# Value products of two attention units in one block, a fourth buffer for turned probabilities, and small tables in another pool

## The chip, the core and the metric

The kernel runs on one NeuronCore of a Trainium2 chip, in one launch. The time is the device time of one execution in microseconds (us); a kernel is run several times and the median counts. The profile is that of one execution, taken by the hardware profiler; its span goes from the first to the last instruction. The engines have their own instruction streams: TensorE (PE in the profile, with its weight loads listed as PEld), VectorE (DVE), ScalarE (ACT), GpSimd (POOL) and SyncE (SP), whose queue issues nearly all DMAs here.

## What is computed

One layer of a diffusion backbone over 1024 latent tokens (a grid of 16 rows of 64 columns) and 256 context tokens, width 1024, all in float32. The normalised and modulated tokens go through one input projection; its output feeds two groups of heads. The first is neighbourhood attention: 8 heads of 64, each query sees a window of 8 rows by 16 columns around it and all context keys in one softmax. The second is a gated delta scan: 4 heads of 128, in two directions, in chunks. Both are gated, put side by side, and sent through the output projection.

```python
def row_block(r):                       # one grid row of queries
    k_win = k_rows[:, :, col_idx]
    v_win = v_rows[:, :, col_idx]
    s_loc = jnp.einsum('bchd,bicjhd->bhcij', q_r, k_win) + bias
    s_ctx = jnp.einsum('bchd,bnhd->bhcn', q_r, k_ctx)
    p = softmax(concatenate([s_loc, s_ctx]))
    return (jnp.einsum('bhcij,bicjhd->bchd', p_loc, v_win)
            + jnp.einsum('bhcn,bnhd->bchd', p_ctx, v_ctx))
...
y = concatenate([o_na * silu(na_z), o_g * silu(g_z)]) @ w_out
x = x + gate * rmsnorm(y, g_post)
```

## The kernel before

The kernel goes through five stages. The first (`phase0`, L194) loads the small tables and the first weights, makes the modulation vectors and the first projections. The second (`phase2`) and third (`phase_a2`) run the other projections, the short convolutions and the preparation of the delta scan. The fourth, `phase_b` (L1492), runs the attention and the scan together. The last, `phase4`, is the output projection; it takes in the tail of the scan.

**Attention.** A unit is 128 queries (8 rows by 16 columns) of two heads; there are 32 units (`units`, L621: 4 pairs of heads, 2 halves of the grid, 4 column groups). The loop of `na_attn` (L665) takes one head of one unit per step, so 64 steps and three more. In step i it does, in this order:
- `na_scores`: the products of queries and keys into the one PSUM tile `sc` (L751 for context, L754 for the window), the masking and row maximum on VectorE (L758), the exponential on ScalarE (L759);
- from step 3 on, in every odd step, `values` (L625), which calls `na_values` for one unit: products of the turned probabilities of both heads with the values, into `po`. One head writes partitions 0 to 63, the other 64 to 127, by half-width tiles of the array (`tile_position=(0, hb)`): 4 products for the context (L784) and 6 for the window (L789). After every fourth unit the sum is multiplied into the gate (L632) and the reciprocal of the softmax sums is spread out (L634 to L639);
- a part of the scan;
- `na_turn` for the step before: five transposes on TensorE into `tc` (L768) and `tr` (L772), copied by ScalarE to `tcx` (L770) and `tl` (L775), of which there are three buffers each;
- after every fourth unit `end`, which turns the reciprocals and multiplies again (L645, L647);
- another part of the scan.

**The scan.** `delta_step` (L1222) has three parts for each step of both directions: L1242 (product with the state) with y on VectorE (L1244); L1260 (product with y) with vn on ScalarE (L1263, L1265); L1271 (update of the state) and, for the outputs, L1249 and L1282. Each needs the result of the one before. The loop in `phase_b` (L1503 to L1506) places just under two such parts in each step of the attention.

**What sets the order.** The matmuls of the attention and scan are chained to each other in program order by `pe` (L594), so their order on TensorE is that of the code. The other engines' order comes from a planner, which simulates the program. Buffers are given out per pool and tag: a tile waits until the readers of the tile that had its place are done.

**Pools.** `cp` (left) and `np` (right) live through the whole kernel; `hp` (left) holds the normalised tokens and is given back after the third stage; `nw` (left) holds the attention's small tiles and opens after that. The constant table `c128` has the identity, two triangles for running sums (`tri_u`, `tri_l`, used in `gate_prep`, L990) and a selector (`sel`).

Of the kernel before, what the change touches and what calls it, by code (L numbers as in the profile page):

```python
# [11 lines left out]
F32 = mybir.dt.float32  # L12
# [8 lines left out]
P = 128  # L21
# [18 lines left out]
def host_consts():  # L40
    ident = np.eye(P, dtype=np.float32)
    i = np.arange(P)
    tri_u = (i[:, None] <= i[None, :]).astype(np.float32)
    tri_l = (i[:, None] >= i[None, :]).astype(np.float32)
    masks = []
    a = np.arange(P) // 16
    c = np.arange(P) % 16
    for rt in range(2):
        r = 8 * rt + a
        rs = np.clip(r - 4, 0, 8)  # L50
        krow = 4 * rt + np.arange(12)
        rok = (krow[None] >= rs[:, None]) & (krow[None] < rs[:, None] + 8)
        for ct in (0, 1, 3):
            q = 16 * ct + c
            cs = np.clip(q - 8, 0, 48)
            kcol = KCOL0[ct] + np.arange(NCOLS[ct])
            cok = (kcol[None] >= cs[:, None]) & (kcol[None] < cs[:, None] + 16)
            ok = rok[:, :, None] & cok[:, None, :]
            m = np.where(ok, np.float32(0), np.float32(NEG))
            masks.append(m.reshape(P, 3, 4, -1).transpose(0, 1, 3, 2).reshape(P, -1))  # L60
    t = np.arange(S)
    row = (t // 64).astype(np.float32)
    col = (t % 64).astype(np.float32)
    inv = np.float32(10000.0) ** (-np.arange(0, 64, 2, dtype=np.float32) / np.float32(64))
    inv = inv.astype(np.float32)
    ar = (row[:, None] * inv[None]).astype(np.float32)
    ac = (col[:, None] * inv[None]).astype(np.float32)
    cr, sr, cc, sc = (f(z.astype(np.float64)).astype(np.float32)
                      for z, f in ((ar, np.cos), (ar, np.sin), (ac, np.cos), (ac, np.sin)))
    tok = lambda z: z.reshape(8, P, -1).transpose(1, 0, 2).reshape(P, -1)  # L70
    rope = np.concatenate([tok(np.concatenate([cr, cc], 1)), tok(np.concatenate([-sr, sr, -sc, sc], 1))], 1)
    sel = (i[:, None] % 32 == np.arange(2)[None, :]).astype(np.float32)
    c128 = np.concatenate([ident, tri_u, tri_l, sel], axis=1)
    return {
        "c128": np.ascontiguousarray(c128),
        "masks": np.concatenate(masks, axis=1).astype(ml_dtypes.bfloat16),
        "rope": np.ascontiguousarray(rope),
    }
# [63 lines left out]
class K:  # L142
# [31 lines left out]
    def setup(self, ctx):  # L174
        tc, nc, I = self.tc, self.nc, self.I
        self.cp = ctx.enter_context(tc.tile_pool(name="cp", bufs=1, side="left"))
        self.dp = ctx.enter_context(tc.tile_pool(name="dp", bufs=1, space=DRAM))
        cp = self.cp
        c128 = cp.tile([P, 3 * P + 2], F32, name="c128")
        nc.sync.dma_start(c128, I["c128"])  # L180
        self.ident = c128[:, 0:P]
        self.tri_u = c128[:, P:2 * P]
        self.tri_l = c128[:, 2 * P:3 * P]
        self.sel = c128[:, 3 * P:3 * P + 2]
        self.cols = cp.tile([P, 117], F32, name="cols")
        self.gg_dram = self.dp.tile([1, D], F32, name="gg_dram")
        self.nwh = cp.tile([P, 1], F32, name="nwh")
        self.ones = cp.tile([P, 1], F32, name="ones")
        nc.gpsimd.memset(self.ones, 1.0)
        self.mhalf = cp.tile([P, 1], F32, name="mhalf")  # L190
        nc.gpsimd.memset(self.mhalf, -0.5)


    def phase0(self):  # L194
        tc, nc, I = self.tc, self.nc, self.I
        cp = self.cp
# [3 lines left out]
        self.chl = self.hp.tile([P, KC, CT], F32R, name="chl")  # L200
        np_, vp, ps = self.np, self.vp, self.ps
        self.v_dram = self.dp.tile([4, 64, 4, 512], F32, name="v_dram")
        self.gates = np_.tile([P, 10, 16], F32, name="gates")
        self.vcx = np_.tile([P, 2, 512], F32, name="vcx")
        with tc.tile_pool(name="p0", bufs=1, side="right", reuse_waits="tile") as p0:
            vt = p0.tile([P, P], F32, name="vt")
# [4 lines left out]
            nc.vector.tensor_copy(cols, pv[:, :117])  # L211
            nc.vector.tensor_scalar(self.nwh, cols[:, 116:117], 0.5, None, ALU.mult)
            th = p0.tile([P, 16], F32, name="th")
            sc = self.sc = self.np.tile([P, 8, 32], F32, name="sc")
            nc.gpsimd.memset(sc, 0.0)
            nc.scalar.activation(th, cols[:, 0:16], AF.Tanh, scale=0.5)
            nc.vector.tensor_scalar(th, th, 0.5, 0.5, ALU.mult, ALU.add)
# [139 lines left out]
            gates = [self.gate_proj(vp, ps, 0, 1536, gate_w(1536))]  # L357
# [39 lines left out]
        f = self.I["rpbp"]  # L397
# [88 lines left out]
    def values(self, pool, w, n, tiles):  # L486

        for t in tiles:
            sel = self.nat_tok(t - 2) if t >= 2 else self.ctx_tok(t)
            pv = self.ps.tile([P, 512], F32, name=f"pv{t}_{n}", tag="pj", bufs=3)  # L490
            self.mm_tok(pv[:, :264], w, 0, 264, sel)
            self.values_out(t, n, pv)
# [106 lines left out]
    def na_attn(self, na, ps):  # L599


        nc = self.nc
# [62 lines left out]
        for i in range(2 * len(units) + 3):  # L665
            if i < 2 * len(units):
                j, hh = divmod(i, 2)
                p, rt, ct = units[j]
                if (ct, hh) == (0, 0):
                    sums[p, rt] = self.nw.tile([P, 4, 2], F32, name=f"sums{p}_{rt}", tag="sums", bufs=2)  # L670
                scores[i] = self.na_scores(ps, p, rt, ct, hh, pairs[p], sums[p, rt])
                if p < 3 and (rt, ct, hh) == (0, 2, 0):
                    self.gate = self.scan_loads
                    pairs[p + 1] = load(p + 1)
                    self.gate = None
            if i >= 3 and i % 2:
                values((i - 3) // 2)
            yield
            if 1 <= i <= 2 * len(units):
                turned[divmod(i - 1, 2)] = self.na_turn(ps, *scores.pop(i - 1))  # L680
            if i >= 4 and i % 8 == 2:
                end((i - 4) // 2)
            self.split_piece(1, 2)
            yield
# [78 lines left out]
    def na_turn(self, ps, nm, m, pt):  # L763
        nc = self.nc
        pc = ps.tile([P, 256], F32, name=f"tc{nm}", tag="tc", bufs=1)
        pl = ps.tile([P, 384], F32, name=f"tr{nm}", tag="tr", bufs=1)
        for cc in range(2):
            self.pe(nc.tensor.transpose(pc[:, cc * P:(cc + 1) * P], pt[:, 384 + cc * P:384 + (cc + 1) * P], self.ident))  # L768
        tcx = self.nw.tile([P, 2, P], F32, name=f"tcx{nm}", tag="tcx", bufs=3)
        nc.scalar.copy(tcx.rearrange("p c q -> p (c q)"), pc)  # L770
        for rc in range(3):
            self.pe(nc.tensor.transpose(pl[:m, rc * P:(rc + 1) * P], pt[:, 384 + (rc - 3) * m:384 + (rc - 2) * m],  # L772
                                        self.ident))
        tl = self.nw.tile([P, 384], F32, name=f"tl{nm}", tag="tl", bufs=3)
        nc.scalar.copy(tl[:m, :], pl[:m, :])  # L775
        return tl, tcx

# [779 lines left out]
```

## Time and profile before

| what | us |
|---|---|
| runs: lowest, median, highest | 875.4, 877.32, 1006.16 |
| span of the profiled execution | 869.9 |
| TensorE busy in the span | 824.9 |
| VectorE, ScalarE, GpSimd busy | 502.7, 417.3, 357.3 |

For the profiled execution only its span is listed; the time of a run is measured around it, and the lowest of the runs is 5.5 us above the span. A matmul's busy time overlaps the next one's, so TensorE's busy share says little of how densely it issues; the start times of its instructions do. A row of the timeline merges neighbouring instructions of one line: start, duration of the whole, engine, line, operation, output and inputs, count, and in brackets the idle time of that engine before it and what ended it.

### The profile page before, as it was taken

Reading aid. Unit: us, or ns where it says so; the run is one execution under the profiler, and the core shown is the slowest. Engines: PE = TensorE matmul, PEld = TensorE weight load, DVE = VectorE, ACT = ScalarE, POOL = GpSimd, SP = SyncE. Lnnn points to the kernel's source line nnn. Section 1 sums busy time; section 2 is a strip of 40 time slices with the busy share of each in tenths; the row PEclk is TensorE's granted clock in tenths of the full one; section 3 lists DMA queues with packets and bytes.
Section 4 is the critical chain, followed back from the end, with each engine's and each line's share of the span. In section 5 each row is a group of like instructions: output and inputs, shape, how many; then the busy total and the mean of one; then the engine's idle time right before and its main releaser. Section 6 shows DMA issues by size and latency. Waiting matters only on the chain.

```text
span 869.9 us, 16461 instructions
## 1 busy us (share of the span) xinstructions
PE 824.9 (95%) x6082; PEld 696.4 (80%) x6082; DVE 502.7 (58%) x1051; ACT 417.3 (48%) x1087; POOL 357.3 (41%) x430
## 2 busy tenths in 40 slices
PE   6999999999999989989898999899999999999996
PEld 3678887888788867769786788788898988878885
DVE  3444455536743699859935964456666655653342
ACT  5244334753664643355314334366666667734210
POOL 2224141453462553328262100655757559624110
PEclk9999999999999999989998999699999999999999
DMA  8778352255444825562597569995967925134251
GB/s 340 265 259 295 97 170 88 73 170 168 142 157 154 221 85 170 176 171 81 176 283 226 160 187 290 419 258 149 313 179 262 259 78 191 49 110 133 87 184 69
DMA packets 86054, 159.65 MB, mean 184 GB/s; under 512 B 18373, under 2 KB 45334, under 8 KB 83798
## 3 DMA queue, kind: packets, MB, share of 16 engines
q1 hardware_dynamic: 78486, 144.94, 53.0%
q10 hardware_dynamic: 7488, 13.67, 5.1%
q8 instruction: 48, 0.79, 0.4%
q14 instruction: 32, 0.26, 0.1%
HBM read 109.51 MB, written 52.42 MB: 186 GB/s over the span
## 4 chain that ended last, share of the span: by engine, by line
PE 59%; DVE 16%; DMA 15%; issue 4%; ACT 2%; POOL 2%; SPq 1%; DVEq 0%; POOLq 0%; ACTq 0%
PE py L1369 3%; PE py L1370 3%; PE py L1371 3%; DVE tb L1078 3%; DVE vb L1081 3%; PE pa L1260 2%; PE pz L463 2%; PE pz L468 2%; PE pz L467 2%; PE po L789 2%; DMA wada<-in_w_ada 2%; PE pa L1271 2%; PE po L784 2%; DMA pm_dram<-pm 2%; PE tr L772 2%
## 5 line engine op out<-in xcount | busy, mean ns | idle before, releaser
L759 ACT ACTIVATE pt<-pt,nm 128x544 f32<-128x544 f32 (+1 forms) x64 | 50.5, 790 | 37.5 <-DVE nm L758 37.0
L758 DVE CUSTOM_DVE_ANT_0 pt<-sc,gm 128x544 f32<-128x544 f32 (+1 forms) x64 | 49.4, 771 | 32.2 <-PE sc L754 25.8
L742 POOL TENSOR_TENSOR gm<-gt,mk 128x288 f32<-128x288 f32 (+1 forms) x48 | 46.5, 971 | 29.1 <-DVE nm L758 28.8
L1232 POOL TENSOR_SCALAR kd<-kt,kd 128x128 f32<-128x128 f32 x72 | 42.7, 605 | 20.5 <-PE pa L1271 19.9
L1020 ACT ACTIVATE em<-em,gc 128x128 f32<-128x128 f32 x80 | 25.5, 391 | 34.9 <-DMA em<-gc_dram 29.7
L467 PE MATMUL pz<-hl,wh_gz 128*128 128x512 f32 x96 | 38.6, 402 | 0.0
L463 PE MATMUL pz<-hh,wh_gz 128*128 128x512 f32 x96 | 38.3, 399 | 0.0
L468 PE MATMUL pz<-hh,wl_gz 128*128 128x512 f32 x96 | 38.2, 398 | 0.0
L476 PE MATMUL pv<-wh_nv,hh 128*128 128x264 f32 x128 | 35.5, 296 | 2.0 <-ACT hh L265 1.7
L477 PE MATMUL pv<-wh_nv,hl 128*128 128x264 f32 x128 | 36.8, 292 | 0.0
L1431 DVE TENSOR_TENSOR finv<-py,ggb 128x512 f32<-128x512 f32 x16 | 10.9, 689 | 43.2 <-ACT finv L1430 43.1
L478 PE MATMUL pv<-wl_nv,hh 128*128 128x264 f32 x128 | 35.6, 287 | 0.0
L1274 DVE SCALAR_TENSOR_TENSOR s<-s,egl,pa 128x128 f32<-128x128 f32 x64 | 19.6, 344 | 27.2 <-PE pa L1271 27.2
L1039 POOL TENSOR_SCALAR_AFFINE_SELECT qe<-qe 128x256 f32<-128x256 f32 x32 | 25.5, 800 | 24.1 <-DVE qe L1038 24.1
L887 DVE SCALAR_TENSOR_TENSOR acc_v<-xp_v,cols,acc_v 128x1282 f32<-128x1282 f32 x16 | 29.1, 1817 | 10.9 <-ACT acc_v L885 10.6
L1078 DVE TENSOR_TENSOR tb<-ab,vb 120x31 f32<-120x31 f32 (+15 forms) x62 | 30.2, 487 | 8.7 <-DMA ab<-ab_dram 7.1
L1137 POOL COPY tm<-ld 32x320 f32<-32x320 f32 x16 | 7.4, 464 | 65.0 <-DMA tm_dram<-tm 27.1
L1430 ACT ACTIVATE finv<-py 128x512 f32<-128x512 f32 x16 | 9.5, 597 | 48.6 <-PE py L1371 30.5
L1238 POOL TENSOR_SCALAR vb<-v,beta 128x128 f32<-128x128 f32 x40 | 24.2, 604 | 20.4 <-DVE y L1244 17.2
L772 PE MATMUL tr<-c,pt 128*96 128x128 f32 (+1 forms) x192 | 31.8, 275 | 0.0
L1035 DVE SCALAR_TENSOR_TENSOR pm<-pk,beta,em 128x128 f32<-128x128 f32 x80 | 23.5, 342 | 14.0 <-PE pk L1028 10.9
L770 ACT COPY tcx<-tc 128x256 f32<-128x256 f32 x64 | 23.4, 366 | 16.2 <-PE tc L768 15.8
(432 smaller groups left out, 2852.7 us busy)
## 6 DMA issues: line engine op xcount, KB each, us to landing
wada<-in_w_ada SPq DMA_DIRECT2D x16, 512.0 KB
em<-gc_dram SPq DMA_DIRECT2D x20, 256.0 KB
pm_dram<-pm SPq DMA_DIRECT2D x20, 256.0 KB
tm_dram<-tm SPq DMA_DIRECT2D x8, 640.0 KB
kk<-qk_dram SPq DMA_DIRECT2D x16, 320.0 KB
tm<-tm_dram SPq DMA_DIRECT2D x4, 1280.0 KB
kq_dram<-kq SPq DMA_DIRECT2D x4, 1152.0 KB
kq<-kq_dram SPq DMA_DIRECT2D x4, 1152.0 KB
```

What stands on the lines that cost most here:

```text
L463: r = nc.tensor.matmul(ps, wh, xh, start=(k == 0), stop=False)
L467: nc.tensor.matmul(ps, wh, xl, start=False, stop=False)
L468: nc.tensor.matmul(ps, wl, xh, start=False, stop=(k == KC - 1))
L476: nc.tensor.matmul(ps, xh, wh, start=(k == 0), stop=False)
L477: nc.tensor.matmul(ps, xl, wh, start=False, stop=False)
L478: nc.tensor.matmul(ps, xh, wl, start=False, stop=(k == KC - 1))
L742: r = nc.gpsimd.tensor_tensor(self.gm[hh][:, 384 - n:384].rearrange("p (n c r) -> p n c r", c=nco, r=4), gv, self.mk[:, mo:mo + n].rearran ...
L758: nc.vector.tensor_tensor_reduce(pt[:, 384 - n:], sc[:, 512 - n:768], gm[:, 384 - n:], -1.0, 3.0e38, ALU.add, ALU.min, nm)
L759: self.last_exp = nc.scalar.activation(pt[:, 384 - n:], pt[:, 384 - n:], AF.Exp, bias=nm, scale=-1.0, accum_out=sums[:, ct, hh:hh + 1]).in ...
L772: self.pe(nc.tensor.transpose(pl[:m, rc * P:(rc + 1) * P], pt[:, 384 + (rc - 3) * m:384 + (rc - 2) * m], self.ident))
L1078: nc.vector.tensor_tensor(t3, bc(ab[:, 0:m, m:m + 1], [r, m, n]), bc(vb[:, m:m + 1, m:], [r, m, n]), ALU.mult)
L1232: r = nc.gpsimd.tensor_scalar(kd[d], kt_[:, t, :], self.kd[:, h, d, t:t + 1], None, ALU.mult)
```

## The change

- `na_attn`: `values` is no longer called for one unit in every odd step from 3 on, but for two units, one behind the other, in every fourth step: steps 5, 9, 13 up to 65.
- `na_turn`: four buffers instead of three for `tcx` and `tl` (2.5 KB more per partition).
- The constant table is laid out as identity, selector, triangles. The first two are loaded into `cp`, the triangles by a DMA of their own into `hp`. `gates` and the silu vector `sc` move from `np` to `hp`. (`cp` gives up 1 KB per partition, `np` 1.6 KB, `hp` takes 2.6 KB.)

```diff
-    c128 = np.concatenate([ident, tri_u, tri_l, sel], axis=1)
+    c128 = np.concatenate([ident, sel, tri_u, tri_l], axis=1)
...
-        c128 = cp.tile([P, 3 * P + 2], F32, name="c128")
-        nc.sync.dma_start(c128, I["c128"])
+        c128 = cp.tile([P, P + 2], F32, name="c128")
+        nc.sync.dma_start(c128, I["c128"][:, :P + 2])
         self.ident = c128[:, 0:P]
-        self.tri_u = c128[:, P:2 * P]
-        self.tri_l = c128[:, 2 * P:3 * P]
-        self.sel = c128[:, 3 * P:3 * P + 2]
+        self.sel = c128[:, P:P + 2]
...
-        self.gates = np_.tile([P, 10, 16], F32, name="gates")
+        self.gates = self.hp.tile([P, 10, 16], F32, name="gates")
+        tri = self.hp.tile([P, 2 * P], F32, name="tri")
+        nc.sync.dma_start(tri, I["c128"][:, P + 2:])
+        self.tri_u, self.tri_l = tri[:, :P], tri[:, P:]
...
-            sc = self.sc = self.np.tile([P, 8, 32], F32, name="sc")
+            sc = self.sc = self.hp.tile([P, 8, 32], F32, name="sc")
...
-            if i >= 3 and i % 2:
+            if i >= 5 and i % 4 == 1:
+                values((i - 5) // 2)
                 values((i - 3) // 2)
...
-        tcx = self.nw.tile([P, 2, P], F32, name=f"tcx{nm}", tag="tcx", bufs=3)
+        tcx = self.nw.tile([P, 2, P], F32, name=f"tcx{nm}", tag="tcx", bufs=4)
...
-        tl = self.nw.tile([P, 384], F32, name=f"tl{nm}", tag="tl", bufs=3)
+        tl = self.nw.tile([P, 384], F32, name=f"tl{nm}", tag="tl", bufs=4)
```

## The prediction

> **What bounds the kernel now.** I read the page first, for the share of each engine, then the windows of the attention stage, then its timeline, and last the waits of TensorE's weight loads in it.
>
> ```profile
> span 869.9 us, 16461 instructions
> PE 824.9 (95%) x6082; PEld 696.4 (80%) x6082; DVE 502.7 (58%) x1051; ACT 417.3 (48%) x1087; POOL 357.3 (41%) x430
> ...
> core 0: us, PE busy (x) PEld busy (x) DVE busy (x) ACT busy (x) POOL busy (x), PEclk, DMA share, GB/s
> 552.00:781.00 229.00, 220.38 (x2022) 199.37 (x2021) 136.11 (x414) 144.61 (x443) 140.82 (x191) 0.99 0.66 200
> ```
>
> The value products run only between 552 and 781 us of the span. There TensorE is busy for 220.38 of 229.00 us at a granted clock of 0.99, VectorE for 136.11, ScalarE for 144.61, GpSimd for 140.82. So the stage is TensorE's instruction stream, and what shortens it is time in which that stream issues nothing. The other three are busy for about 60%; they cannot bound the stage by throughput, but a late answer of theirs can stop the stream. The order of the attention's and scan's matmuls is written by hand, so the change of the loop moves them exactly as written.
>
> The stream around one block of value products (unit 24/25, the first row is a scores product of the step before, which has no such block):
>
> ```profile
> 631.05 0.30 PE L754 MATMUL sc<-kk,ql 128*128 128x288 f32 x1
> 631.18 0.66 PE L1260 MATMUL pa<-y,tm 128*128 128x128 f32 x4
> ...
> 633.93 0.30 PE L754 MATMUL sc<-kk,ql 128*128 128x288 f32 x1
> 634.16 0.42 PEld L784 LDWEIGHTS po<-tcx,vcx 128*64 128x64 f32 x8 [0.17 <-ACT o L1286]
> 634.16 0.66 PE L784 MATMUL po<-tcx,vcx 128*64 128x128 f32 x8
> 634.65 0.83 PE L789 MATMUL po<-tl,vv 96*64 96x128 f32 x12
> 635.40 0.52 PEld L1242 LDWEIGHTS pa<-s,kq 128*128 128x128 f32 x4 [0.17 <-DVE o L1290]
> 635.40 0.71 PE L1242 MATMUL pa<-s,kq 128*128 128x128 f32 x4
> ```
>
> Read the start times: from the last scores product to the next matmul it is 0.13 us without a block (631.05 to 631.18), 0.23 us into a block of half-width tiles (633.93 to 634.16). The weight loads stand still for 0.17 us at the way in, and again 0.17 us at the way out (the brackets), each time beside a releaser that has nothing to do with the operands. I take the two gaps, 0.34 us, as the price of entering and leaving the 128x64 tiles once. The block itself lasts from 634.16 to 635.40, 1.24 us.
>
> **The change, part by part.** 1. *Half the blocks.* Today there are 32 blocks of 20 value instructions (4 products of context, 6 of the window, two instructions each), one in every second step. Afterwards there are 16 blocks of 40. No matmul is added or dropped; 16 entries and exits go: 16 x 0.34 = 5.4 us off the stream. Bounds: 0 if the gap is something else (a rival below), 5.4 by these rows.
>
> 2. *The operands of a block.* Waits of the weight loads in the stage (who waited for what: us in total, times, longest us), with the group of L784 above them:
>
> ```profile
> L784 PEld LDWEIGHTS po<-tcx,vcx 128*64 128x64 f32 x256 | 13.4, 136 | 8.5 <-ACT tcx L770 2.1 <-ACT vn L1265 1.6 <-issue 1.5
> ...
> PEld pa L1260 <- DVE y L1244: 5.6, 11, 0.7
> PEld po L784 <- ACT tcx L770: 2.1, 4, 0.7
> PEld sc L751 <- DVE nm L758: 1.9, 3, 1.3
> ...
> PEld po L784 <- ACT tl L775: 1.0, 4, 0.3
> PEld po L784 <- ACT pt L759: 1.0, 2, 0.7
> PEld pa L1271 <- ACT vn L1263: 1.0, 2, 0.6
> ```
>
> A block's last operand is the turned probability of the step just before, copied out of PSUM by ScalarE. The three ScalarE rows that carry it (the two copies, and the exponential that stands ahead of them) make 2.1 + 1.0 + 1.0 = 4.1 us in 10 entries; less 0.17 us each for the entry itself, 2.4 us are real waits. In a double block the first unit's operands are two steps old and its 1.24 us cover the second unit's. So this wait goes: 2.4 us off. Bounds: 0, and 8.5 - 32 x 0.17 = 3.1 us, all idle time before L784 that is not entry.
>
> 3. *The bare steps.* What takes the place of the removed blocks is the cost. A step without a block gives VectorE and ScalarE less time. Two steps side by side, first a bare one, then one with a block:
>
> ```profile
> 651.63 0.29 PE L754 MATMUL sc<-kk,ql 128*128 128x288 f32 x1
> 651.64 0.54 PEld L1242 LDWEIGHTS pa<-s,kq 128*128 128x128 f32 x4
> ...
> 652.32 0.71 DVE L758 CUSTOM_DVE_ANT_0 pt<-sc,gm 128x544 f32<-128x544 f32 x1
> 652.96 0.34 DVE L1244 SCALAR_TENSOR_TENSOR y<-pa,nsc,v 128x128 f32<-128x128 f32 x1
> 653.22 0.34 DVE L1244 SCALAR_TENSOR_TENSOR y<-pa,nsc,vb 128x128 f32<-128x128 f32 x1
> 653.36 0.56 PEld L1260 LDWEIGHTS pa<-y,tm 128*128 128x128 f32 x4 [0.68 <-DVE y L1244]
> ...
> 634.38 0.72 DVE L758 CUSTOM_DVE_ANT_0 pt<-sc,gm 128x544 f32<-128x544 f32 x1
> 636.13 0.34 DVE L1244 SCALAR_TENSOR_TENSOR y<-pa,nsc,v 128x128 f32<-128x128 f32 x1
> 636.52 0.56 PEld L1260 LDWEIGHTS pa<-y,tm 128*128 128x128 f32 x4
> ```
>
> In the bare step the scan's first product (L1242) follows the scores at once. VectorE first masks the scores (L758, 0.71 us), and only then makes the scan's y (L1244); the scan's next product (L1260) waits for it, 0.68 us. In the step with a block (634.38 on) the masking ran under the values, y was made as soon as its product was there, and L1260 shows no wait. Today 33 of the 64 steps of scores have no block. Afterwards blocks stand only in every fourth step, so 16 steps (3, 7, ... 63) become bare. The scan has three parts per step of its own and nearly two are placed in each loop step, so L1242 comes first in about one bare step in three: 16 / 3 = 5.3 more. At the mean of the row, 5.6 / 11 = 0.51 us, that is 2.7 us. The two other answers that a bare step can wait for, the masking before the next scores (1.9 us in 3, of which one of 1.3 lies alone; I take 1.9 - 1.3 = 0.6) and the scan's vn on ScalarE (1.0 us), make 1.6 us over these 33 steps, so 0.8 us over 16 more. Together 3.5 us on. Bounds: 0, where VectorE and ScalarE find the time in the longer pause of the double block, and 16 x 0.68 = 10.9 us, where every new bare step waits as the one shown.
>
> 4. *Four buffers.* Two units wait for their products at once, so four turned tiles live. The copy into a buffer comes behind transposes that stand after the block on the same in-order stream; the block has read the buffer by then. No new wait: 0. A fifth live tile never arises.
>
> 5. *PSUM and the end.* The products of a row of four units still accumulate in one tile and are read at the same step; what follows them (the next unit's first block) comes two steps later than today, which only loosens it. At the end the block of unit 30 moves from step 63 to step 65, behind the last turn:
>
> ```profile
> 763.68 0.66 PE L784 MATMUL po<-tcx,vcx 128*64 128x128 f32 x8
> ...
> 773.63 0.66 PE L784 MATMUL po<-tcx,vcx 128*64 128x128 f32 x8
> ...
> 775.80 0.88 PE L789 MATMUL po<-tl,vv 96*64 96x128 f32 x12
> ...
> 777.85 1.77 DVE L1316 TENSOR_TENSOR o<-o,rq_y_o 128x512 f32<-128x512 f32 x1
> 779.54 0.68 DVE L632 TENSOR_TENSOR zs<-po,zs 128x512 f32<-128x512 f32 x1
> 780.37 0.63 PE L645 MATMUL prt<-c,rb 128*128 128x128 f32 x4 [1.66 <-DVE zs L632]
> ```
>
> The last block ends at 775.80 + 0.88 = 776.68, but VectorE reads it only at 779.54, behind L1316. Another 1.24 us before it is covered by that 2.86 us, and the stream is shorter by as much ahead of it. 0, with bounds 0 and +1.24.
>
> 6. *Small tables.* The table with the identity is loaded in two DMAs, and the second (128 KB of triangles) is one more issue on SyncE's queue, ahead of the vectors and of every load of the first phase:
>
> ```profile
> 0.79 0.39 SPq L180 DMA_DIRECT2D c<-in_c  x1
> 1.23 0.43 SPq L207 DMA_DIRECT2D vt<-in_vecs  x1
> ...
> 3.51 0.43 PE L209 MATMUL pv<-c,vt 117*128 117x117 f32 x1 [3.51 <-DMA vt<-in_vecs]
> 11.44 2.24 PE L294 MATMUL par<-wada,sc 128*32 128x512 f32 x8 [0.21 <-DMA wada<-in_w_ada]
> ```
>
> One issue takes 0.43 us, and everything behind it on that queue starts so much later: the vectors that L209 waits for, and the w_ada loads that the first products wait for at 11.44. The bytes are the same. I take +0.4 us; bounds 0 and +0.4. GpSimd's and ScalarE's queues are not passed. A page of the Trainium skill speaks for more: DMA: Bandwidth & Descriptors, in its part on the life of a DMA, gives every transfer a fixed cost of about 2.0 us beside its bytes at 436 GB/s. By it, if the new load stood whole on the chain, my estimate for it would be 2.3 us and the sum 1.9 us worse. The trace agrees with the size and not with the place: the vectors are there 3.51 - 1.23 = 2.28 us after their issue, but the table issued 0.44 us earlier was there by the same moment, so transfers run side by side and only the issue adds. Moving the gates and the silu vector to another pool changes no instruction.
>
> **The sum:** -5.4 - 2.4 + 3.5 + 0 + 0 + 0.4 = -3.9 us against the profiled span of 869.9, so 866.0. No time of the profiled execution is listed beside its span; the median of the runs, 877.32, lies 7.4 us above it, the lowest, 875.4, 5.5 us. I hang the difference on the median: 873.4, about 0.4% faster. What a measurement of this kernel can tell from no change is about 2%, 17.5 us.
>
> **The rivals.** *Bare steps cost nothing.* The double block leaves VectorE and ScalarE a pause of 2.5 us in every fourth step in which they catch up; for it speaks their 60% of busy time, against it the 0.68 us above, which is order on VectorE and not load. -5.4 - 2.4 + 0.4 = -7.4: 869.9.
>
> *Bare steps cost more* (the other side). Three bare steps now follow each other, and VectorE's masking stands before y in each of them: at the 0.68 us of the bare step shown, in all 16, it is +10.9 - 7.8 + 0.4 = +3.5: 880.8, slower than before. It decides from 7.4 / 16 = 0.46 us per new bare step. Against it: L1242 stands first in only a third of them. To pass 2% it would take (17.5 + 7.4) / 16 = 1.56 us per step, more than any wait of the stage's rows above.
>
> *The change does not do what it says.* If the 0.17 us gaps belong to the operands or to this particular PSUM tile, a block of 40 keeps a gap in its middle, nothing of the 5.4 us is saved: -2.4 + 3.5 + 0.4 = +1.5: 878.8. Against it the way out, where the gap stands before L1242, whose operands are a state and a key that no value product touches. A page of the Trainium skill, TensorEngine Tiling (Array Packing), under its key properties, says that a change of the tiling mode, not of the tile, drains TensorE; by that rule this rival falls and the 5.4 us stand. The two gaps of 0.17 us agree with it as far as a trace without a double block can.
>
> **How the numbers follow.** My forecast has a chance of 0.55, bare steps at nothing 0.15, bare steps dearer 0.2, gaps that stay 0.1. The predicted time is the first's, 873.4. The range goes from 868.0 (the second, with 3.1 instead of 2.4 us of operand waits, 869.2, and 1.2 us for the runs' own spread) to 882.0 (the third, 880.8, and the 1.24 us of the end). By these cases faster by over 2% would need more than all idle time priced above: 0.03. Slower by over 2% is the far end of the third: 0.04. Within 2%: 0.93.
>
> **What would show it.** In the changed profile: half as many idle gaps of 0.17 us before L784, and 40 value instructions without a gap in their middle (step 1); no row of L784 waiting for tcx or tl (step 2); L1260 waiting for y in about 16 places instead of 11 and some 2.7 us more (step 3); TensorE's idle time at the end as it is (step 5); the vectors' issue 0.4 us later (step 6). The prediction is wrong if the stage from the first scores to the last turned row does not get shorter by 3 to 6 us, or if time moves outside that stage, which only a new order of the other engines by the planner could do.

## The result and the profile after

| kernel | median us (runs) | ratio to the kernel before, 95% interval |
|---|---|---|
| before, measured beside it | 872.54 (7) | |
| changed | 879.12 (7) | 1.0077 [1.0054, 1.0100] |

The change makes the kernel about 0.8% slower, 6.6 us. That is under the 2% that the prediction set as the bound of a visible difference, but the interval leaves no doubt of the sign. The prediction said 0.4% faster.

The page and the windows of the changed kernel, for the stage from the first scores to the last turned row:

```profile
span 877.4 us, 16456 instructions
PE 829.0 (94%) x6082; PEld 704.2 (80%) x6082; DVE 504.6 (58%) x1051; ACT 417.6 (48%) x1087; POOL 359.5 (41%) x430
...
552.00:789.00 237.00, 223.12 (x2030) 203.68 (x2029) 137.64 (x416) 144.75 (x443) 141.91 (x191) 0.97 0.64 195
```

Each engine runs as many instructions as before, but the stage is 8 us longer (237 against 229 us), TensorE stands still for 13.9 us in it instead of 8.6, and its granted clock is 0.97 instead of 0.99. By three marks, the first scores product, the first product of the last step of scores and the end: 552.4, 763.0 and 869.9 before; 553.1, 771.7 and 877.4 after. So +0.7 us ahead of the stage, +8.0 in it, -1.2 behind it.

What the change was meant to do, it did. One double block in the timeline (start, duration, engine, line; from here on the rows of a timeline or of a list of waits are picked out, in their order):

```profile
640.31 0.29 PE L756 MATMUL sc<-kk,ql 128*128 128x288 f32 x1
640.54 0.66 PE L786 MATMUL po<-tcx,vcx 128*64 128x128 f32 x8
641.02 0.83 PE L791 MATMUL po<-tl,vv 128*64 128x128 f32 x12
641.68 0.61 PE L786 MATMUL po<-tcx,vcx 128*64 128x128 f32 x8
642.12 0.83 PE L791 MATMUL po<-tl,vv 96*64 96x128 f32 x12
642.87 0.71 PE L1244 MATMUL pa<-s,kq 128*128 128x128 f32 x4
```

The 40 instructions have no idle time in their middle: the second unit's L786 starts 0.66 us behind the first's L791, like any two lines of one block. From 640.54 to 642.87 it is 2.33 us, where two blocks of before took 2 x 1.24 us, each with a way in of its own ahead of it.

The waits of the weight loads in the stage show what it cost instead (waited for: us in total, times, longest):

```profile
PEld pa L1262 <- DVE y L1246: 11.0, 20, 1.0
PEld po L786 <- issue: 3.9, 17, 0.4
PEld pos L1251 <- DVE o L1292: 3.6, 4, 1.4
PEld sc L753 <- DVE nm L760: 2.2, 4, 1.3
PEld ot L1321 <- POOL o L1313: 2.1, 1, 2.1
```

No row of L786 waits for tcx or tl any more, and it has 17 short idle times. But the wait for y has doubled (5.6 us in 11 before), and two waits are new: for the scan's output o on VectorE, and for the product on GpSimd that ends a scan.

The steps of the loop can be compared one by one: from the first scores product of a step to that of the next, less 1.09 us for each unit of value products and 0.345 us for each block in it. Both come from the steps: a double block makes a step 1.09 us longer than a single one (the median of 15 steps), and in steps 7 and 15, where nothing waits, a single block makes it 1.44 us longer than none, so a block costs some 0.35 us beside its products.

| steps | changed less before, us |
|---|---|
| the newly bare ones up to the last but one (3, 7, ... 59, 15 steps) together | +5.6 |
| old bare ones: 8, 20, 24 | +1.3, +2.5, +1.9 |
| old bare ones: 16, 32, 48 | +0.3, +0.5, +0.7 |
| 21 (with a double block, at half clock) | +1.0 |
| all 63 | +13 |

Against these 13 us stand the 5 us of saved blocks. More than half of the loss (7.5 us) is in steps that had no block before either, and those the prediction had not priced at all. Two entries of the sum can't simply be put down to the double blocks: step 55 (+1.8) and step 2 (+0.6). Against the same trace of before, step 55 is 1.3 to 1.6 us longer in runs 1, 9, 11, 14 and 15 below, and step 2 is 0.8 to 1.0 us longer in runs 11, 13 and 14, all with single blocks: in these two steps that trace was a short one. Step 24, in the timeline of the changed kernel:

```profile
634.89 1.13 POOL L744 TENSOR_TENSOR gm<-gt,mk 128x384 f32<-128x384 f32 x1
634.98 0.19 ACT L761 ACTIVATION_READ_ACCUMULATOR pt<-pt,nm 128x1 f32 x1
635.20 0.86 DVE L635 TENSOR_SCALAR rs<-sums 128x8 f32<-128x8 f32 x1 [0.45 <-ACT pt L761]
635.50 0.30 PE L756 MATMUL sc<-kk,ql 128*128 128x288 f32 x1
635.97 0.34 DVE L1246 SCALAR_TENSOR_TENSOR y<-pa,nsc,v 128x128 f32<-128x128 f32 x1
636.37 0.62 PEld L1262 LDWEIGHTS pa<-y,tm 128*128 128x128 f32 x4 [0.81 <-DVE y L1246]
636.76 0.71 DVE L760 CUSTOM_DVE_ANT_0 pt<-sc,gm 128x544 f32<-128x544 f32 x1
637.61 0.29 DVE L1292 TENSOR_TENSOR o<-pos,o 128x128 f32<-128x128 f32 x1
637.96 0.52 PEld L1251 LDWEIGHTS pos<-s,kq 128*128 128x128 f32 x4 [0.97 <-DVE o L1292]
```

The doubling of the softmax sums, rs (eight numbers per partition), stands ahead of y. It waits for the exponential's sums (0.45 us) and then takes 0.86 us. It ends at 636.06, 0.04 us behind the end of GpSimd's gm (634.89 + 1.13 = 636.02). TensorE waits for y, and 1.6 us later again for o. In the trace of before the same instruction stands one step earlier, between the scan's two state updates, and meets only the end of gm:

```profile
628.48 1.14 POOL L742 TENSOR_TENSOR gm<-gt,mk 128x384 f32<-128x384 f32 x1 [1.43 <-DVE nm L758]
629.48 0.17 DVE L634 TENSOR_SCALAR rs<-sums 128x8 f32<-128x8 f32 x1
629.56 0.33 DVE L1274 SCALAR_TENSOR_TENSOR s<-s,egl,pa 128x128 f32<-128x128 f32 x1
```

Nobody wrote that move: with the value block gone from step 23, the planner found another order for VectorE. In step 20 it did the same on GpSimd. First the changed kernel, with the granted clock (the last but two of the windows' numbers) behind it, then before:

```profile
618.24 1.18 POOL L1234 TENSOR_SCALAR kd<-kt,kd 128x128 f32<-128x128 f32 x2
619.39 1.90 POOL L1313 TENSOR_TENSOR o<-o,rq_y_o 128x1024 f32<-128x1024 f32 x1
621.34 0.66 PE L1321 MATMUL ot<-c,o 128*128 128x128 f32 x4 [1.95 <-POOL o L1313]
...
622.00:624.00 2.00, 2.00 (x11) 1.56 (x11) 0.75 (x1) 0.85 (x2) 0.72 (x2) 0.50 1.00 231
```

```profile
615.85 1.90 POOL L1311 TENSOR_TENSOR o<-o,rq_y_o 128x1024 f32<-128x1024 f32 x1
617.72 1.18 POOL L1232 TENSOR_SCALAR kd<-kt,kd 128x128 f32<-128x128 f32 x2
617.93 0.60 PE L1319 MATMUL ot<-c,o 128*128 128x128 f32 x4
```

The two kd stand ahead of the product o now; TensorE waits 1.95 us for it, and is then granted half its clock.

### The profile page after: what moved, and what is told of

The parts are those of the page before. It is cut to its first block, busy times and chain, and to the rows that moved or that the text cites. A ratio compares the mean times of both kernels' runs of the same rounds, so it can differ in the third digit from the quotient of the medians.

```text
span 877.4 us, 16456 instructions
## 1 busy us (share of the span) xinstructions
PE 829.0 (94%) x6082; PEld 704.2 (80%) x6082; DVE 504.6 (58%) x1051; ACT 417.6 (48%) x1087; POOL 359.5 (41%) x430
## 4 chain that ended last, share of the span: by engine, by line
PE 67%; DVE 16%; DMA 10%; issue 3%; POOL 2%; ACT 2%; SPq 1%; DVEq 0%; POOLq 0%; ACTq 0%
PE py L1371 3%; PE py L1372 3%; PE py L1373 3%; DVE tb L1080 3%; PE pz L464 3%; PE pz L468 3%; PE pz L469 3%; PE pa L1262 2%; DVE vb L1083 2%; PE po L791 2%; DMA pm_dram<-pm 2%; PE po L786 2%; PE tr L774 2%; PE sc L756 2%; PE pos L1251 2%
## 5 line engine op out<-in xcount | busy, mean ns | idle before, releaser
L889 DVE SCALAR_TENSOR_TENSOR acc_v<-xp_v,cols,acc_v 128x1282 f32<-128x1282 f32 x16 | 29.0, 1814 | 10.9 <-ACT acc_v L887 10.6
L1433 DVE TENSOR_TENSOR finv<-py,ggb 128x512 f32<-128x512 f32 x16 | 10.9, 689 | 41.5 <-ACT finv L1432 41.5
```

## The experiments

Three theories stood at the start. **A**: the loss is the new order on VectorE and GpSimd. **B**: three bare steps in a row starve the scan's own chain, whatever the order. **C**: the moved tables and the buffers cost. Later expectations name their own. "Before" is measured beside each set of runs and lies at 872.3 to 873.1 us.

**1. The tables and buffers alone.** The changed kernel with the loop of before:

```diff
-            if i >= 5 and i % 4 == 1:
-                values((i - 5) // 2)
+            if i >= 3 and i % 2:
                 values((i - 3) // 2)
```

> The small tables in the other pool and the four buffers, with the loop of before (one unit's value products in every odd step). Theory A (the loss comes from where VectorE's and GpSimd's small operations stand once the blocks are doubled): the attention stage as before, the first phase up to 0.7 us later, time within 1 us of the kernel before. Theory C (tables or buffers cost by themselves, through the first phase or through waits for memory): 3 us or more slower than before, and the doubled blocks are innocent.

Measured: 876.45 us, 1.0048 [1.0029, 1.0066], 4 us: C's number. The stage lasts 211.5 us (before 210.6), so nearly all of it lies outside. This was a surprise, and runs 7, 11, 14 and 15 follow it up. In the profiled execution the first scores come 2.3 us later than before, and the part behind the last scores is 1.4 us longer, with half the clock from 785.3 to 788.7 us. The traces of runs 9 and 15 have that second stretch too, and their times are those of before, so it is no answer.

**2. The order on GpSimd.** The changed kernel with the two kd of step 2 of the next scan held behind the product o:

```diff
+                if h and i == 2:
+                    self.order(r, self.o_done)      # r: the kd, o_done: the product L1313
```

> The changed kernel, with one order added on GpSimd: at the end of a head the product of the outputs with their norm (1.9 us) stands ahead of the two kd products of the next head's third step, as it did before the change. Theory A: the 2.1 us wait of the transposes (ot) in step 20 goes, and with it the 3.4 us at half clock that follow it: 2 to 3.5 us faster than the changed kernel, about 876 us. Theory B (three bare steps in a row starve TensorE, whatever the order): no more than 1 us faster.

Measured: 879.22 us, 1.0085 [1.0052, 1.0117]. The stage fell from 218.6 to 215.9 us; step 20 loses 0.8 instead of 2.5 us, and step 21 ran at full clock. So the order costs what A said, inside the stage. But the total kept nothing of it, as B said. In that profile the first scores came 5.3 us later than in the changed kernel's, which hides it there; why the median of four runs shows no gain stays open.

**3. Both orders.** As 2, and rs held behind the product of the value sums, which puts it behind y and o:

```diff
+            gated = nc.vector.tensor_tensor(row(p, rt), po[p, rt]..., row(p, rt), ALU.mult)
-            nc.vector.tensor_scalar(rs, sums[p, rt]..., 2.0, None, ALU.mult)
+            self.order(nc.vector.tensor_scalar(rs, sums[p, rt]..., 2.0, None, ALU.mult), gated.ins.name)
```

> As the one with the order on GpSimd, and on VectorE the doubling of the softmax sums (rs) stands behind the product that reads the value sums, so in the step with a double block and no longer in the bare step ahead of it. Theory A: the waits of steps 8, 16, 24, 32, 48 and 55 go as well, 5 to 6 us more: about 870 us, 2 to 3 us faster than before the change. Theory B: within 1.5 us of the changed kernel, 878 us.

Measured: 879.13 us, 1.0081 [1.0054, 1.0108], stage 215.2. Steps 8, 24 and 48 lose 0.8, 0.9 and 0.3 instead of 1.3, 1.9 and 0.7, but the sum hardly moved. A's 870 was missed: these two orders are not the whole loss.

**4. The kernel before, with the order of after for rs.** rs and its reciprocal moved into the bare step, behind the last state update and ahead of y:

```diff
+            if i >= 8 and i % 8 == 0:
...
+                r = nc.vector.tensor_scalar(rs, sums[p, rt]..., 2.0, None, ALU.mult)
+                self.order(r, self.last_s)
```

> The kernel before, its blocks in every odd step, with the doubling and reciprocal of the softmax sums put into the bare step after the fourth unit's last scores (steps 8, 16, ...), ahead of that step's y on VectorE. Theory A: the place alone costs: 3 to 6 us slower than before, with L1260 waiting for y or the output products for o in those steps. Theory B: the place costs nothing without three bare steps in a row: within 1 us of before.

Measured: 872.5 us, 1.0006 [0.9980, 1.0032]; no step differs by over 0.25 us. The place of rs alone costs nothing: there it met GpSimd's kd rather than gm in five of eight places, and took 0.16 to 0.27 us in seven. That points to the meeting with gm as what costs; runs 5 and 6 test it.

**5. An addition for the doubling.** In the changed kernel rs became the sum of the sums with themselves:

```diff
-            nc.vector.tensor_scalar(rs, sums[p, rt]..., 2.0, None, ALU.mult)
+            nc.vector.tensor_tensor(rs, t, t, ALU.add)       # t: the sums
```

> The changed kernel with the doubling of the softmax sums (rs, 128x8) written as the sum added to itself, a two-operand addition, instead of a multiplication by a constant; no engine's order changes. Theory A (the constant multiplication is held up by a running GpSimd table addition, since it ended 0.03 us behind the end of gm in steps 8, 24, 48 and 55, and an addition is not): the eight take 0.16 to 0.2 us each, 1.4 in all in place of 3.6, the products y behind them come 0.4 to 0.7 earlier in four steps, and the time falls by 1.5 to 3 us, to 876 to 877.5. Rival B (they wait for the exponential's sums, or any VectorE instruction is held up so): the eight still take 0.2 to 0.9 us and the time stays at 879.

Measured: 879.2 us, 1.0071 [1.0047, 1.0095]. The addition is held up just the same (instruction, count, ns min/median/max, first and last start), so the first form of the explanation fell:

```profile
L636 DVE TENSOR_TENSOR rs<-sums x8: 164/391/853, 579.0 to 776.6; 128x8 f32<-128x8 f32 x8
```

That it is gm and not the exponential shows in the trace of run 1, step 55, where the sums had been there for 0.16 us when rs started:

```profile
738.50 0.18 ACT L760 ACTIVATION_READ_ACCUMULATOR pt<-pt,nm 128x1 f32 x1
738.53 1.13 POOL L743 TENSOR_TENSOR gm<-gt,mk 128x384 f32<-128x384 f32 x1
738.84 2.07 DVE L635 TENSOR_SCALAR rs<-sums 128x8 f32<-128x8 f32 x1
739.62 1.26 POOL L712 TENSOR_TENSOR early_ql<-raw,early_qh 128x512 fp32r<-128x512 f32 x1
740.82 0.34 DVE L1245 SCALAR_TENSOR_TENSOR y<-pa,nsc,vb 128x128 f32<-128x128 f32 x1
741.21 0.30 PEld L1261 LDWEIGHTS pa<-y,tm 128*128 128x128 f32 x2 [1.88 <-DVE y L1245]
```

rs sits through the rest of gm and through the whole next GpSimd addition, and ends at 740.91, 0.03 us behind it (739.62 + 1.26 = 740.88). The Trainium skill has the reason: "SBUF — State Buffer", in the section on its two sides, says that VectorE and GpSimd share a pair of ports as an exclusive lock, which a VectorE instruction in a two-port mode or with two SBUF inputs needs, and that the loser blocks for the whole of the other's instruction. The ends that agree to 0.04 us bear it out for gm and the additions, though not every GpSimd instruction blocked rs for its whole length (the last section has two that did not), and by it the addition, with two SBUF inputs, could not have helped. The products y, which read PSUM, ran wholly beside gm in 18 places of the changed kernel's trace and took 0.34 to 0.35 us as ever.

**6. No doubling.** The reciprocal reads the sums, and GpSimd's spreading multiplies by 0.5:

```diff
-            nc.vector.tensor_scalar(rs, sums[p, rt]..., 2.0, None, ALU.mult)
-            nc.vector.reciprocal(rs, rs)
+            nc.vector.reciprocal(rs, sums[p, rt]...)
...
-            nc.gpsimd.tensor_copy(rb[j], bc(rs.unsqueeze(2), [P, 8, 64]))
+            nc.gpsimd.tensor_scalar(rb[j], bc(rs.unsqueeze(2), [P, 8, 64]), 0.5, None, ALU.mult)
```

> The changed kernel without the doubling rs: the reciprocal reads the sums and GpSimd's spreading of it multiplies by 0.5, so that VectorE has no instruction between the sums and the reciprocal that a GpSimd table addition can hold up (the reciprocal took 0.19 us in every step of both traces). Theory A: steps 8, 24 and 48 lose 0.5 to 0.8 us of their excess each (of 1.26, 1.93 and 0.72), and the stage falls from 218.6 to about 216.5; total 876.5 to 878. Rival B (the hold-up is covered by the masking behind it): stage within 0.7 of 218.6, total 879.

Measured: 877.12 us, 1.0069 [1.0049, 1.0088], in A's range; stage 215.6 instead of 218.6, steps 8, 24 and 48 down by 0.5, 1.0 and 0.3. Another 1.3 us of the 3.0 are the half clock in step 21: it is gone, though the standstill ahead of it is still there (1.94 us), so this part can't be put down to rs. The reciprocal is never held up, though gm runs beside seven of its eight:

```profile
L635 DVE RECIPROCAL rs<-sums x8: 192/203/204, 581.3 to 775.3; 128x8 f32<-128x8 f32 x8
```

So the hold-up is shown, in place and in size: 1.7 us of the stage.

**7. The triangles by another queue.** As run 1, the triangles fetched by GpSimd's queue:

```diff
-        nc.sync.dma_start(tri, I["c128"][:, P + 2:])
+        nc.gpsimd.dma_start(tri, I["c128"][:, P + 2:])
```

> The tables and the four buffers as in the change, the value blocks as before (one unit in every odd step), and the two triangles fetched by GpSimd's queue instead of SyncE's. The planner then lays TensorE's order in the merging of the inverses (530 to 545 us) as in the kernel before, apart from the triangles' name. Theory A (the 4 us that the tables cost come from that order: the last merge ends 1.6 to 2.3 us later in all four kernels with the moved tables): the first scores come within 1 us of 552.4 and the time is 872 to 874. Theory B (the moved tables or the fourth buffers themselves cost, by where they lie or by the second transfer): the time stays at 876 to 877.

Measured: 877.86 us, 1.0063 [1.0039, 1.0088]: A's number failed. The stage is 210.6 us, that of before, so in the stage of this execution tables and buffers cost nothing. The loss lies in the hand-over to it. In SyncE's queue the last write of a merged inverse now stood behind a read of one (128x2560) that it preceded before; the chain of waits has that write at

```profile
542.62 10.44 DMA tm_dram<-tm
```

and the first scores came at 559.3. So the order there seems to cost, but this run had a third order, not that of before, and doesn't show it by itself.

**8. Three orders in the changed kernel.** The addition of 5, the order of 2, and in bare steps the masking behind both y:

```diff
+            if not (i % 4 != 1):
+                self.last_nm = None
...
+                if self.last_nm:
+                    self.order(self.last_nm, r.ins.name)      # last_nm: the masking, r: y
```

> The changed kernel with three edits: the doubling as an addition, the scan end's product ahead of the next two kd on GpSimd, and in the steps without a value block VectorE's masking of the scores ordered behind the two products y. Theory A (a step without a value block waits because y stands behind 0.75 us of masking, and so the loss of the stage is VectorE's order): TensorE's waits for y fall from 17 us to under 6, the attention stage from 218.8 to 205 to 210 us, and the time to 868 to 872. Rival B (the loss is the scan's chain itself, and masking that comes 0.7 us later makes the exponential and the turns late instead): the stage stays over 214 and new waits for the exponential or the turns appear; 877 to 882.

Measured: 874.69 us, 1.0026 [1.0004, 1.0048]; stage 213.2. The wait for y is gone (0.5 us on TensorE, from 5.9), but a new one took its place, so the stage missed A's 205 to 210, and the total A's 868 to 872:

```profile
PE pos L1259 <- DVE o L1300: 5.2, 12, 0.8
PE sc L757 <- DVE nm L764: 2.5, 5, 0.9
```

The scan's addition into o had come behind the masking too.

**9. The same for the kernel before** (the addition, and the masking behind y in even steps):

```diff
+            if not (i % 2 == 0):
+                self.last_nm = None
```

> The kernel before with two edits: the doubling as an addition, and in the even steps, which have no value block, VectorE's masking ordered behind the two products y. Theory A: TensorE's waits for y (5.6 + 3.0 us) fall by 4 to 6 us, in steps 6, 8, 16, 22, 30, 44, 46 and 60 by 0.35 to 0.6 each; 866 to 869. Rival B (masking later makes the exponential and the turns late): 872 to 876.

Measured: 871.34 us, 0.9996 [0.9976, 1.0015]. Steps 8 and 46 gained 0.5 and 0.7, steps 20, 37 and 58 lost 0.6, 1.2 and 0.6; in the profiled run the hold-up in step 55 took 2.08 us, against 0.51 in the trace of before. A's 866 to 869 was missed, and B's 872 to 876 as well.

**10. All orders in the changed kernel.** No doubling (6), the order of 2, and the masking behind y and behind the last addition into o:

```diff
+            elif self.last_nm and self.last_o and i < 2 * len(units):
+                self.order(self.last_nm, self.last_o)
```

> The changed kernel with the doubling taken out, the scan end's product ahead of the next kd on GpSimd, and in the steps without a value block the masking behind the two products y and behind the scan's last addition into o. Theory A (what is left in the version before, 5.2 us of waits for o in 12 places and 1.9 us in step 24, is again VectorE's order): waits for o fall under 2 us, the stage from 213.2 to 207 to 210, the total to 869 to 872, about 3 under what the three orders gave (874.7). Rival B (the masking, now 1 us later, sends the wait to the scores or the exponential): the stage stays at 212 to 215, waits for nm over 4 us.

Measured: 870.76 us, 0.9981 [0.9963, 0.9999], 8.4 us under the change as made. In its stage, 210.3 us long, the wait for o is 0.4 us. A held in its total and in its waits for o; the stage came 0.3 us above its range.

**11. One more transfer, nothing moved.** The kernel before with its table fetched in two parts into the same tile; every engine then has the order of run 1:

```diff
-        nc.sync.dma_start(c128, I["c128"])
+        nc.sync.dma_start(c128[:, :P + 2], I["c128"][:, :P + 2])
+        nc.sync.dma_start(c128[:, P + 2:], I["c128"][:, P + 2:])
```

> The kernel before with one edit: the table of constants is fetched by two transfers (130 and 256 columns) into the same tile, as many as the change issues. No table moves, three buffers stay, the value blocks stay; the planner's order on every engine becomes that of the kernel with tables alone (876.45). Theory A (the cost of the moved tables is the order of the hand-over around 530 to 560 us, which the planner lays otherwise as soon as SyncE has one more transfer at the start): 875.5 to 877.5, the last merge's products 1.5 to 2.5 us later against what went before. Rival B (where the tables lie, or the fourth buffers): 872 to 873.

Measured: 873.75 us, 1.0004 [0.9985, 1.0023]. The merge was later by what A said, but the total rose by 0.7 us, within its interval of none, not by 4.

**12. All orders in the kernel before** (those of 10 in VectorE's order, in even steps; single blocks, three buffers, tables in place):

```diff
+            if not (i % 2 == 0):
+                self.last_nm = None
+            elif self.last_nm and self.last_o and i < 2 * len(units):
+                self.order(self.last_nm, self.last_o)
```

> The kernel before with the same edits: the doubling taken out and, in the even steps, the masking behind the products y and the last addition into o. Theory A: the waits for y (8.6 us) fall to under 3 and the 2.1 us that the doubling lost in step 55 in the version before do not come back; stage 206 to 208.5 instead of 210.6, total 868 to 870. Rival B: what y gains the scores lose; 871 to 873.

Measured: 870.31 us, 0.9980 [0.9966, 0.9995]; stage 208.1. The least time of all, 0.3 us above A's range.

**13. All orders, moved tables, single blocks.** The edits of 12 in the kernel of run 1; against run 10 the double blocks are missing, and the order of 2 that only they need:

```diff
-            if i >= 5 and i % 4 == 1:
-                values((i - 5) // 2)
+            if i >= 3 and i % 2:
                 values((i - 3) // 2)
```

> The tables and four buffers of the change, single value blocks as before, and the three edits of the version with double blocks that gave 870.76 (no doubling, masking behind y and behind o in the even steps). Against that version only the double blocks differ. Theory A (the 16 saved blocks are worth their 5 us once the steps without a block no longer wait): 874 to 876, and the double blocks gain 4 us. Rival B (the steps without a block lose what the saved blocks gain, even with the orders mended, since the scan's own chain fills them; the two stages are 208.1 and 210.3 with the end 1.2 shorter): 870 to 872.5, stage 208 to 209.

Measured: 871.75 us, 0.9989 [0.9974, 1.0004]; stage 209.2. B holds: the double blocks are worth 1.0 us by the medians, less than the intervals can tell from none. The windows of the two stages, double blocks first:

```profile
555.37:765.66 210.29, 203.13 (x1903) 188.55 (x1903) 126.37 (x388) 140.18 (x425) 142.11 (x184) 0.98 0.69 207
...
551.78:760.93 209.15, 204.10 (x1904) 187.09 (x1903) 126.86 (x388) 140.23 (x425) 141.99 (x184) 0.98 0.70 208
```

With double blocks TensorE is busy for 1.0 us less and stands idle for 2.1 us more. By steps, priced as in the table above, 6.3 us are still lost (39 alone 1.1, 24 0.9, 3 and 51 0.6 each) against 15 saved blocks of 0.345: 4.3 us in the newly bare steps and 2.7 in the old bare ones, less 0.7 in those with double blocks. These are single traces; by the medians the two kernels can't be told apart.

**14. Moved tables, three buffers** (run 1 with three buffers, the same order on every engine):

```diff
-        tcx = self.nw.tile([P, 2, P], F32, name=f"tcx{nm}", tag="tcx", bufs=4)
+        tcx = self.nw.tile([P, 2, P], F32, name=f"tcx{nm}", tag="tcx", bufs=3)      # tl too
```

> The tables moved as in the change, three buffers, single value blocks; the order on every engine is that of the run with tables and four buffers. Theory A (the moved tables cost what that run lost): 875.5 to 877.5. Rival B (the fourth buffers do): 872.5 to 874, like the split transfer alone.

Measured: 874.49 us, 1.0012 [0.9993, 1.0031], between the two.

**15. The gates and sc alone moved** (no new transfer; the order of before on every engine):

```diff
-        self.gates = np_.tile([P, 10, 16], F32, name="gates")
+        self.gates = self.hp.tile([P, 10, 16], F32, name="gates")      # sc too
```

> The kernel before with only the gates and sc moved to the pool of the activations; no transfer is added, and the order on every engine is that of before. Theory A (only what changes the order, or the triangles' own tile, costs): 872 to 873.5. Rival B (where the gates and sc lie costs): 874.5 to 876.5.

Measured: 873.07 us, 0.9999 [0.9978, 1.0021]: A, their place costs nothing.

**The hand-over, put together.** From a gate product late in the third stage (the one that starts at 530.12 us in the trace of before) to the first scores:

| order there | us from that product to the first scores |
|---|---|
| of before: before, runs 4, 9, 12, 15 | 22.3 to 22.8 |
| one more transfer at SyncE: changed kernel, runs 1, 2, 3, 5, 6, 8, 10, 11, 13, 14 | 23.9 to 24.5 |
| run 7 | 25.9 |

Eleven kernels with one more transfer are 1.1 to 2.2 us slower there than five without, whether a table moved or not (run 11). That is shown. Why run 1 loses 4.1 us in its median, and runs 14 and 11, with the same order on every engine, 1.4 and 0.7, is not settled: the fourth buffers, other addresses or chance would each fit, and run 1 was measured on another chip than runs 11 and 14, each beside the kernel before. The stage says nothing for the buffers: it was not longer with them in run 7 (210.6 us), and without them it was 212.5 and 212.9 us in runs 11 and 14. Even run 15, with the order of before on every engine, had 211.5, so a stage of one execution is no better than a microsecond or two; 1.3 to 1.6 us in each of these three traces are the hold-up in step 55.

## Why the prediction was wrong

- **Step 1, half the blocks, -5.4: right.** 17 idle times before L786, none in the middle of a block; 15 blocks saved between the first and the last scores, at 0.345 us 5.2 us. The sixteenth pair, behind the last scores, saves nothing: products of the output projection stand between its two units (the second starts at 782.74).
- **Step 2, the operands, -2.4: right in kind.** The rows of tcx, tl and pt are gone; no run shows the 2.4 us by themselves.
- **Step 3, the bare steps, +3.5: the step that failed.** It counted only the new bare steps (+5.6 in 15 of them, 1.8 of that in step 55, where the trace of before was a short one), and took VectorE's and GpSimd's order as given everywhere. The prediction's last part named a new order by the planner as the way for time to move outside the stage; the order moved inside it too, and the sum held nothing for either. The old bare steps lost 7.5 us that were not in the sum. Of the loss of the stage, rs against gm carries 1.7 us (run 6), kd ahead of o 2.7 us (run 2, with 1.3 of half clock in it), and the masking ahead of y and o the remaining 4, by difference: with all of them mended (run 10) the stage fell from 218.6 to 210.3.
- **The upper bound of step 3, 0.68 us for each of 16 steps, was no bound** for what the stage can lose: 13 us over all steps against its 10.9, since a wait can appear in any step whose neighbour changes.
- **Even with the orders mended, the steps cost 6.3 us (runs 10 and 13), not 3.5,** 4.3 of it in the new bare ones. So the rival "bare steps cost more" was right in sign and place; its price (3.5 us slower) was too low, for it held no new order either.
- **Step 4, four buffers, 0:** no wait shows in the stage; run 1 against run 14 leaves up to 2 us open.
- **Step 5, PSUM and the end, 0:** the part behind the last scores became 1.2 us shorter: TensorE's wait for the gate product (`prt`, L645, 1.7 us in the prediction's rows) is 0.5 us now. The sign was not seen, but nothing was lost.
- **Step 6, the tables, +0.4: mis-sized.** The issue is there (0.42 us). What it moves is the planner's order at the hand-over, 530 us later, at 1.1 to 2.2 us. That moving the gates and sc costs nothing was right (run 15). The larger price by the Trainium skill's page "DMA: Bandwidth & Descriptors", in its section on the anatomy of one DMA, came out at a like size by accident: the products that wait for the vectors start 0.26 us later (3.77 against 3.51; at 3.8 to 4.7 in the other traces with that transfer on SyncE's queue), not 2 us.
- **"The gaps stay" fell:** the double block has no gap in its middle, and the Trainium skill's page that spoke against this rival, "TensorEngine Tiling (Array Packing)", in its key properties, agrees with the trace.
- The time, 879.12, lies inside the range given only by luck: the base of 877.32 was the median of three runs, one of them 1006; nineteen to twenty-nine later runs put it at 872.3 to 873.1. Hung on the 872.54 measured beside the change, the same range would have ended at 877.2.

## What to carry to other kernels

A block of work on the busiest engine is also the cover under which the other engines answer; before moving it, list for every step that loses it, and for its neighbours, what those engines hold in their queues ahead of the answer, and price that order, not only the work. Where a planner lays those queues, price a new order as a cost of its own: one more transfer of 0.4 us shifted another stage by 1 to 2 us. Order by hand what feeds the critical engine: here y and o ahead of the masking, the scan's product ahead of kd, and no doubling that a GpSimd addition can hold up. Together that was worth 8.4 us to the change and 0.2% to the kernel before, and the double blocks 1.0 us on top, which is less than the runs can tell from nothing.

## What the hardware showed unexpectedly

- An instruction of eight numbers per partition took 2.07 us beside two GpSimd additions, and a waiting VectorE instruction lost the port again to the second of them (739.62, 0.78 us behind its own start). Beside GpSimd's kd, which multiplies by one number per partition, the same instruction took 0.16 to 0.27 us, and in run 3 it took 0.16 us inside a GpSimd power of eight numbers per partition that ran for 1.67 us. So not every GpSimd instruction blocks it. In run 15, with every engine's order as before, it took 2.10 us where the trace of before has 0.51: a shift of some 0.4 us in its start against gm's goes with it (0.28 against 0.66 us behind), and 1.6 us of scatter between executions hang on it.
- A standstill of TensorE of 1.95 us can be enough for half the clock, and need not be: in the changed kernel it read 0.50 from 622.0 and was back at full in the window from 625.5, while the same standstill in run 6 (1.94 us) left the clock at full. Near the end, a standstill of 1.6 to 1.7 us ahead of the last `prt` products was followed by half the clock in runs 1, 9 and 15, and not in the traces of before and run 12. The Trainium skill, "TensorE: Matmul & The Clock Gate", in its table of the two states, asks for about 3.4 us of idling first; the duration of the slow stretch, about 3.4 us, agrees with its window, the idling does not.
